# Hybrid trunk layer: which instructions behind the second hand-written order are tied to the order of the source

## The chip, the core and the metric

One core of one Trainium2 chip runs the kernel. Its engines work side by side, each in the order of its own instruction stream: TensorE (PE in the profile, its weight loads PEld) multiplies, VectorE (DVE), ScalarE (ACT) and GpSimd (POOL) do the elementwise work, and SyncE (SP) issues the DMA transfers. The metric is the device time of one execution in microseconds, the median over runs.

## The reference

One layer of a decoder trunk over 1024 tokens of width 1024, all in float32. The first half projects the normed input, runs stick-breaking attention (8 heads) beside a convolution module, and adds an output projection to x. The second half, in which the change lies, is a feed-forward network with a causal convolution of width 3 on its gate:

```python
h = rms_norm(x, norm2_g[layer])
gate, val = jnp.split(h @ w_up[layer], 2, axis=-1)
gate = jax.nn.silu(causal_depthwise_conv(gate, ffn_dw_w[layer], ffn_dw_b[layer]))
x = x + (gate * val) @ w_down[layer]
```

`w_up` is 1024 x 5632 and `w_down` 2816 x 1024.

## The kernel before

**Precision.** A float32 operand is split into a rounded high part (ScalarE, line 383: a cast) and the rest (VectorE or GpSimd, line 384: the operand minus its high part). A product of two operands is three matmuls (lines 387 to 389): high with high, high with low, low with high.

**The up-projection.** The 2816 gate columns and the 2816 value columns are worked in 22 blocks, f = 0 to 21. Block f takes 128 gate columns and 128 value columns, each 1024 long, that is a 2 x 2 arrangement: a11 and a12 are the two halves (512 rows each) of the gate columns, a21 and a22 those of the value columns. With the token side B cut in the same way, seven products take the place of eight. Besides a11, a12 and a22, four sums are operands; in `sums_up` they are made on GpSimd: S1 = a21 + a22 (line 1829), S3 = a11 - a21 (line 1830, written over a21), S2 = S1 - a11 (line 1831, over a11) and S4 = a12 - S2 (line 1835, over a12). Each is then split. In `up`, seven products of 12 matmuls each go to PSUM banks, and VectorE adds them into the gate g and the value v (lines 2000 to 2008; the first is copied by ScalarE, line 1999). Then come the gate's convolution (ScalarE at line 2009, two VectorE instructions at line 2011), Silu (ScalarE, line 2013), the product with the value (VectorE, line 2014), and a store to DRAM (line 2015). The profile calls the operands a11, a12, a22 `a` and the sums `aS`, the products `u` and `u_S`, the loaded weights `rawu`, S1 before its split `s`.

**Buffers.** Weights of even blocks are loaded to the two buffers raw0 and raw1, those of odd blocks to three buffers of the tag xt (line 1805). The gate half of block 1 is the exception: it lies in raw0. So the gate half of block 2 goes to raw0 when S4 of block 1 is split, and the value half of block 2 to raw1 when S4 of block 0 is split. Products use six PSUM banks of the tag z, those of a11 and a12 in the loop two of the tag bank.

**What sets the order.** The program is put in order when it is built, by a list scheduler with a timing estimate: an instruction that it holds ready may go ahead of one that stands earlier in the source. Two stretches are exempt: a `Plan` object emits its operations by a list of numbers (`ORDERS`), and `in_order` then ties each instruction of an engine to the one before it, which needs no semaphore but fixes the order of the stream. The second plan holds the output projection, the second norm, all seven products of block 0 with their additions (line 1928), and of block 1 the gate's load, the splits of a11 and a12 and their two products. It ends at line 1986. Behind it stands the loop over f:

```python
for f in range(NF):
    if f + 1 < NF:
        raw_next = load_up(f + 1)
    up(f, A)
    if f + 1 < NF:
        A = sums_up(f + 1, raw_next)
    if f == 0:
        in_order(start_at, last_planned, ORDERED[1:])
```

The call in its last line covers what the first turn emits: of `up(0)` only the convolution, Silu, product and store are left, and of `sums_up(1)` the four sums and the splits of S2, S1, S3, S4 and a22, in this order. On VectorE, ScalarE and GpSimd these are tied to each other in the order of the source and behind the last planned instruction of their engine. TensorE's and SyncE's streams are not tied there, nor is anything of block 2 and later, which the scheduler may put among or before them.

Of the kernel before, what the change touches and what calls it, by code (L numbers as in the profile page):

```python
# [40 lines left out]
ORDERED = (mybir.EngineType.PE, mybir.EngineType.DVE, mybir.EngineType.Activation, mybir.EngineType.Pool)  # L41
# [103 lines left out]
class Plan:  # L145
# [36 lines left out]
    def add(self, cost, *args):  # L182
        if not isinstance(cost, dict):
            cost, args = {cost: args[0]}, (lambda eng, f=args[1]: f(),) + args[2:]
        op = Plan.Op()
        op.shares = "DVE2" in cost
        op.cost, op.emit, op.key = {e.rstrip("2"): c for e, c in cost.items()}, args[0], args[1]
        op.after = list(args[2]) if len(args) > 2 else []
        op.takes = list(args[3]) if len(args) > 3 else []
        op.end, op.engine, op.n, op.moves = None, None, len(self.ops), [Plan.ROWS]  # L190
        self.ops.append(op)
        return op
# [77 lines left out]
def kernel(  # L270
# [21 lines left out]
    nc = tc.nc  # L292
# [169 lines left out]
    def part_of(big_tile, i, words):  # L462
        return big_tile[:, i * words:(i + 1) * words]

    def in_order(start_at, last=None, engines=ORDERED):
        last = {} if last is None else last
        for ins in nc.cur_bb.bb.instructions[start_at:]:
            if ins.engine in engines:
                if ins.engine in last:
                    tc.add_manual_dep(ins, last[ins.engine].name, mybir.DependencyInfo(  # L470
                        mybir.DependencyClass.NoSync, mybir.DependencyReason.DATA), reason="planned order")
                last[ins.engine] = ins
        return last

    start_at = len(nc.cur_bb.bb.instructions)
    g1 = []
# [796 lines left out]
    for h, half in [(h, half) for h in range(H) for half in range(2)]:  # L1273
# [38 lines left out]
        for g in (2 * half, 2 * half + 1):  # L1312
# [47 lines left out]
            last = None  # L1360
            if g % 2 == 0:
                po, pd = plan.token("o"), {}
            for sp in range(g + 1):
# [50 lines left out]
                last = add("PE", 480, products, k, [c] + v2 + ([last] if last else [prev_last] if g % 2 else []))  # L1414
# [203 lines left out]

    plan.run(ORDERS[0])
    in_order(start_at)  # L1620
    conv_ctx.close()
    ps_ctx.close()
# [18 lines left out]
    start_at = len(nc.cur_bb.bb.instructions)  # L1641
# [154 lines left out]
    def load_up(f):  # L1796

        both = []
        for b in (0, DFF):
            if f == 1 and b == 0:  # L1800
                both.append(next_raw[0])
                continue
            both.append(op.tile([P, ND, P], F32, tag="xt", name=f"rawu{f}_{b}", bufs=3) if f % 2 else
                        raw([P, ND, P], F32, f"rawu{f}_{b}"))
            nc.sync.dma_start(both[-1], w_up_k[:, :, b + f * P:b + (f + 1) * P])
        return both

    def sums_up(f, raws):

        A = {}  # L1810

        def both(name, src):
            if f == 1 and name in A_next:
                A[name] = A_next[name]
                return
            if name in ("11", "22"):
                tag, bufs = {"11": ("v", 2), "22": ("m", 1)}[name]
                t = op.tile([P, 2, 4, P], F32R, tag=tag, name=f"a{name}_{f}", bufs=bufs)
            else:
                t = whl([P, 2, 4, P], F32R, f"a{name}_{f}")  # L1820
            A[name] = (t[:, 0], t[:, 1])
            split(*A[name], src)

        (a11, a12), (a21, a22) = [(raw[:, :4, :], raw[:, 4:, :]) for raw in raws]
        s1 = op.tile([P, 4, P], F32, tag=f"t{f % 2 + 1}", name=f"s1_{f}")
        tt = nc.gpsimd.tensor_tensor
        both("11", a11)
        both("12", a12)
        tt(s1, a21, a22, op=ALU.add)  # L1829
        tt(a21, a11, a21, op=ALU.subtract)  # L1830
        tt(a11, s1, a11, op=ALU.subtract)
        both("S2", a11)
        both("S1", s1)
        both("S3", a21)
        nc.gpsimd.tensor_tensor(a12, a12, a11, op=ALU.subtract)  # L1835
        both("S4", a12)
        both("22", a22)
        return A
# [145 lines left out]
    gv, banks_of, A_next, next_raw = [], {}, {}, []  # L1984
    first_operands(FIRST)
    plan.run(ORDERS[1])
    last_planned = in_order(start_at)
    start_at = len(nc.cur_bb.bb.instructions)

    def up(f, A):  # L1990
        def product(a, b):
            return product_up(f, A, a, b)

        tt = nc.vector.tensor_tensor
        g, v = gv[f % 2], gv[2 + f % 2]
        y = op.tile([P, S], F32, tag="h2", name=f"y{f}", bufs=2)
        g0, g1, v0, v1 = g[:, :HS], g[:, HS:], v[:, :HS], v[:, HS:]
        if f > 1:
            nc.scalar.copy(v0, product("11", "11"))
            tt(g0, product("12", "21"), v0, op=ALU.add)  # L2000
        if f:
            tt(g1, product("S2", "T2"), v0, op=ALU.add)
            tt(v0, product("S3", "T3"), g1, op=ALU.add)
            p5 = product("S1", "T1")
            tt(g1, p5, g1, op=ALU.add)
            tt(v1, p5, v0, op=ALU.add)
            tt(g1, product("S4", "22"), g1, op=ALU.add)
            tt(v0, product("22", "T4"), v0, op=ALU.add)
        nc.scalar.activation(y, g, AF.Identity, scale=par("fw", (KF - 1) * NF + f), bias=par("fb", f))  # L2009
        for j in range(1, KF):  # L2010
            nc.vector.scalar_tensor_tensor(y[:, j:], g[:, :S - j], par("fw", (KF - 1 - j) * NF + f), y[:, j:],  # L2011
                                           op0=ALU.mult, op1=ALU.add)
        nc.scalar.activation(y, y, AF.Silu)
        tt(y, v, y, op=ALU.mult)
        nc.sync.dma_start(act_d[f], y)
# [4 lines that stand above are left out]
        up(f, A)  # L2020
        if f + 1 < NF:
            A = sums_up(f + 1, raw_next)
        if f == 0:
            in_order(start_at, last_planned, ORDERED[1:])

# [117 lines left out]
    for i in range(len(PAIRS)):  # L2145
        for n, name in enumerate(using if i else making):
# [7 lines left out]
            for s in range(4):  # L2154
# [4 lines left out]
                for j, ((ah, al), (bh, bl)) in enumerate(parts):  # L2159
                    first, last = begins and j == 0, j == len(parts) - 1  # L2160
# [42 lines left out]
```

## Time and profile before

| what | value |
| --- | --- |
| median of 3 runs | 1114.94 us (1114.22 to 1115.05) |
| the profiled execution's own time | 1115.21 us |
| its span, first to last instruction | 1112.9 us |
| busy: VectorE | 871.7 us (78%) |
| busy: ScalarE | 586.9 us (53%) |
| busy: GpSimd | 580.6 us (52%) |
| mean granted TensorE clock | 0.995 |
| DMA | 118.00 MB, mean 106 GB/s |

Times inside the kernel are counted from the span's start. The second plan ends, and the loop begins, at about 490 us; the loop's products run to about 900 us, and the down-projection fills the rest. TensorE's busy time and the chain of waits are shown where they are used. In a row of the timeline the first two numbers are start and duration; in square brackets stands how long the engine had been idle before it, and what ended that.

### The profile page before, as it was taken

What the parts mean: (1) busy time and instruction counts of PE and PEld (TensorE: products, weight loads), DVE (VectorE), ACT (ScalarE), POOL (GpSimd) and SP (SyncE); (2) the same over time, 40 slices, a digit from 0 to 9 for tenths busy, and PEclk for the clock granted to TensorE, in tenths of its full rate; (3) what the DMA queues carried; (4) which work ended last, traced back from release to release, by engine and by line L of the source; (5) the groups of instructions that cost most, each with busy time, mean ns of one, the idle gap of its engine ahead of it and who ended that gap; (6) DMA issues with size and microseconds to landing.
All of it is one profiled execution on the core that took longest, in us unless ns stands there. A gap on an engine that the chain in (4) does not pass through costs nothing.

```text
span 1112.9 us, 14818 instructions
## 1 busy us (share of the span) xinstructions
PE 1088.1 (98%) x5258; PEld 905.4 (81%) x5258; DVE 871.7 (78%) x1200; ACT 586.9 (53%) x1050; POOL 580.6 (52%) x496
## 2 busy tenths in 40 slices
PE   8999999999999999979999999999999999999998
PEld 5888878889898887857888888888888888888887
DVE  5488798789989886878876777677777678797785
ACT  6445466676766654734433434333333378676660
POOL 3177889874734324753433133223322189888770
PEclk9999999999999999998999999999999999999999
DMA  7121210343732434522322222213132482403404
GB/s 269 39 57 32 82 58 20 114 152 120 238 87 77 142 122 144 171 57 78 112 79 92 77 95 75 96 62 107 59 96 75 149 324 77 150 21 133 152 2 150
DMA packets 110504, 118.00 MB, mean 106 GB/s; under 512 B 21369, under 2 KB 90208, under 8 KB 110430
## 3 DMA queue, kind: packets, MB, share of 16 engines
q1 hardware_dynamic: 110414, 117.06, 32.0%
q8 instruction: 41, 0.67, 0.3%
q14 instruction: 33, 0.27, 0.1%
q10 hardware_dynamic: 16, 0.00, 0.0%
HBM read 82.43 MB, written 28.31 MB: 100 GB/s over the span
## 4 chain that ended last, share of the span: by engine, by line
PE 86%; POOL 4%; DVE 3%; DMA 3%; ACT 2%; issue 2%; SPq 0%; DVEq 0%; POOLq 0%; ACTq 0%
PE dn L2162 19%; PE u_S L387 7%; PE u_S L388 7%; PE u_S L389 7%; PE u L387 5%; PE u L389 5%; PE u L388 5%; PE po L1403 3%; PE wT L1375 3%; PE qk L387 3%; PE qk L389 3%; PE qk L388 3%; POOL attn L879 2%; PE z L1334 2%; PE z L1335 1%
## 5 line engine op out<-in xcount | busy, mean ns | idle before, releaser
L2162 PE MATMUL dn<-wd,wd 128*128 128x512 f32 x768 | 181.4, 389 | 0.0
L2162 PEld LDWEIGHTS dn<-wd,wd 128*128 128x128 f32 x768 | 144.2, 188 | 29.9
L387 PE MATMUL u_S<-bT,aS 128*128 128x512 f32 x264 | 103.9, 393 | 10.4 <-ACT aS L383 10.4
L388 PE MATMUL u_S<-bT,aS 128*128 128x512 f32 x264 | 103.4, 392 | 0.0
L389 PE MATMUL u_S<-bT,aS 128*128 128x512 f32 x264 | 102.8, 390 | 0.0
L2165 DVE TENSOR_TENSOR c<-dn,c 128x512 f32<-128x512 f32 x120 | 81.5, 686 | 26.7 <-PE dn L2162 26.1
L2067 ACT CAST wd<-rawd 128x512 fp32r<-128x512 f32 x128 | 72.5, 619 | 32.8 <-DMA rawd<-act_d 9.5
L383 ACT CAST aS<-rawu 128x512 fp32r<-128x512 f32 x63 | 38.8, 621 | 93.2 <-PE u_S L389 66.9
L1356 DVE TENSOR_TENSOR_SCAN nb<-nb,one 128x128 f32<-128x128 f32 (+7 forms) x64 | 84.6, 1340 | 0.6 <-ACT nb L1342 0.5
L1829 POOL TENSOR_TENSOR s<-rawu 128x512 f32<-128x512 f32 x21 | 28.8, 1370 | 107.6 <-DMA rawu<-in_w_up_dram 80.8
L2066 ACT COPY whole<-rawd 128x512 f32<-128x512 f32 x110 | 63.4, 586 | 24.2 <-DVE wd L2068 11.6
L1835 POOL TENSOR_TENSOR rawu<-rawu 128x512 f32<-128x512 f32 x21 | 28.9, 1374 | 80.6 <-DVE a L384 80.6
L2068 DVE TENSOR_TENSOR wd<-whole,wd 128x512 fp32r<-128x512 f32 x90 | 59.9, 684 | 13.5 <-ACT wd L2067 6.7
L387 PEld LDWEIGHTS u_S<-bT,aS 128*128 128x128 f32 x264 | 50.0, 190 | 21.7 <-ACT aS L383 11.4
L2011 DVE SCALAR_TENSOR_TENSOR y<-gv,cols_a,y 128x1023 f32<-128x1023 f32 (+1 forms) x44 | 58.3, 1326 | 10.5 <-ACT y L2009 10.4
L383 ACT CAST a<-rawu 128x512 fp32r<-128x512 f32 x61 | 37.7, 621 | 54.3 <-PE u_S L389 33.9
L389 PE MATMUL u<-b,a 128*128 128x512 f32 x168 | 65.5, 390 | 0.0
L387 PE MATMUL u<-b,a 128*128 128x512 f32 x168 | 65.4, 389 | 0.0
L388 PE MATMUL u<-b,a 128*128 128x512 f32 x168 | 65.4, 389 | 0.0
L388 PEld LDWEIGHTS u_S<-bT,aS 128*128 128x128 f32 x264 | 50.1, 190 | 10.3
L389 PEld LDWEIGHTS u_S<-bT,aS 128*128 128x128 f32 x264 | 49.7, 188 | 10.4
L384 DVE TENSOR_TENSOR a<-rawu,a 128x512 fp32r<-128x512 f32 x61 | 45.4, 746 | 16.0 <-ACT a L383 16.0
(382 smaller groups left out, 3204.9 us busy)
## 6 DMA issues: line engine op xcount, KB each, us to landing
rawu<-in_w_up_dram SPq DMA_DIRECT2D x44, 512.0 KB
act_d<-y SPq DMA_DIRECT2D x22, 512.0 KB
rawd<-act_d SPq DMA_DIRECT2D x22, 512.0 KB
rawd<-in_w_down_dram SPq DMA_DIRECT2D x22, 512.0 KB
raw_qk<-in_w_in_dram SPq DMA_DIRECT2D x16, 256.0 KB
rawo<-in_w_out_dram SPq DMA_DIRECT2D x8, 512.0 KB
m<-conv_d SPq DMA_DIRECT2D x16, 256.0 KB
xt<-in_x_dram SPq DMA_DIRECT2D x8, 512.0 KB
```

The costliest lines, as they stand in the source:

```text
L383: nc.scalar.copy(hi, src)
L384: lo_engine.tensor_tensor(lo, src, f32(hi), op=ALU.subtract)
L387: nc.tensor.matmul(ps, a_hi, b_hi, start=first, stop=False)
L388: nc.tensor.matmul(ps, a_hi, b_lo, start=False, stop=False)
L389: nc.tensor.matmul(ps, a_lo, b_hi, start=False, stop=last)
L1356: nc.vector.tensor_tensor_scan(rev, rev, ones_of[0][:, :w], 0.0, op0=ALU.mult, op1=ALU.max)
L2011: nc.vector.scalar_tensor_tensor(y[:, j:], g[:, :S - j], par("fw", (KF - 1 - j) * NF + f), y[:, j:], op0=ALU.mult, op1=ALU.add)
L2066: nc.scalar.copy(whole, src)
L2067: nc.scalar.copy(t[:, 0], src)
L2068: lo_engine.tensor_tensor(t[:, 1], whole, f32(t[:, 0]), op=ALU.subtract)
L2162: nc.tensor.matmul(ps, a[:, tok], b, start=first and m == 0, stop=last and m == 2, skip_group_check=True)
L2165: nc.vector.tensor_tensor(sums[c][s], ps, sums[c][s], op=ALU.add)
```

## The change

The second call of `in_order` is taken out, with the arguments that served it. The instructions of the two plans are tied as before, on all four engines. The first turn of the loop is no longer tied on VectorE, ScalarE and GpSimd: not among its own instructions, and not behind the planned ones. No instruction is added, taken away or altered.

```diff
-    def in_order(start_at, last=None, engines=ORDERED):
-        last = {} if last is None else last
+    def in_order(start_at):
+        last = {}
         for ins in nc.cur_bb.bb.instructions[start_at:]:
-            if ins.engine in engines:
+            if ins.engine in ORDERED:
                 if ins.engine in last:
                     tc.add_manual_dep(ins, last[ins.engine].name, mybir.DependencyInfo(
                         mybir.DependencyClass.NoSync, mybir.DependencyReason.DATA), reason="planned order")
                 last[ins.engine] = ins
-        return last
...
     plan.run(ORDERS[1])
-    last_planned = in_order(start_at)
-    start_at = len(nc.cur_bb.bb.instructions)
+    in_order(start_at)
...
         if f + 1 < NF:
             A = sums_up(f + 1, raw_next)
-        if f == 0:
-            in_order(start_at, last_planned, ORDERED[1:])
```

## The prediction, made before the result was known

> **What bounds the kernel now.** I read the page first, then the waits of TensorE, then a table by windows.
>
> ```profile
> PE 1088.1 (98%) x5258; PEld 905.4 (81%) x5258; DVE 871.7 (78%) x1200; ACT 586.9 (53%) x1050; POOL 580.6 (52%) x496
> ```
>
> TensorE is busy for 98% of the span, so time can only be won where it stands still or runs slowly. Its waits over the whole span (us in total, times, longest) say where:
>
> ```profile
> PE u_S L387 <- ACT aS L383: 10.4, 1, 10.4
> PE v L739 <- DVE lo_v L604: 1.9, 1, 1.9
> ```
>
> One wait is larger than all others, and it lies at the seam that the change touches. The windows (PE busy first, then its clock, DMA share and GB/s at the end):
>
> ```profile
> 492.74:503.33 10.59, 0.16 (x1) 0.00 (x0) 5.38 (x6) 4.75 (x6) 2.48 (x2) 0.69 0.00 0
> 503.33:508.86 5.53, 5.53 (x16) 4.13 (x17) 5.53 (x6) 2.04 (x4) 3.28 (x2) 0.68 0.28 104
> 508.86:899.80 390.94, 390.94 (x1726) 323.85 (x1725) 287.82 (x351) 149.25 (x216) 126.53 (x89) 1.00 0.30 98
> ```
>
> The reader is to see three things. From 492.74, when the next matmul was due, to 503.33 TensorE does nothing. For the next 5.53 us it is busy but slow. And then, over 391 us in which the scheduler alone set the order, it never pauses: 390.94 / 1726 = 0.2265 us a matmul. The chain that ended last shows what filled the hole:
>
> ```profile
> 487.53 5.15 DMA rawu<-in_w_up_dram
> 492.81 1.27 POOL s L1829
> 494.10 0.63 ACT aS L383
> 494.78 0.97 issue
> 495.76 0.69 DVE gv L1928
> 496.47 1.25 ACT y L2009
> 497.74 1.29 DVE y L2011
> 499.06 1.29 DVE y L2011
> 500.42 1.28 ACT L2013
> 501.72 1.06 ACT y L2013
> 502.77 0.52 ACT aS L383
> 503.33 0.79 PE u_S L387
> ```
>
> The last three lines are the point. The cast that TensorE waits for is block 1's first sum, and on ScalarE it stands behind block 0's Silu only because the source has it so; it needs nothing from the gate. The first lines show a second matter: the cast at 494.10 is of a sum S1, yet stands before line 2009. Block 1's casts are tied behind line 2009, so this one is block 2's, which the scheduler put ahead because its estimate held it ready. It waited for the load of 487.53.
>
> **The change part by part.** No instruction comes or goes; only the order is free. What goes is the tie of block 1's casts behind Silu. When could they have run?
>
> ```profile
> 487.46 1.30 POOL L1829 TENSOR_TENSOR s<-rawu 128x512 f32<-128x512 f32 x1
> 488.83 1.30 POOL L1830 TENSOR_TENSOR rawu<-rawu,rawu 128x512 f32<-128x512 f32 x1
> 490.21 1.29 POOL L1831 TENSOR_TENSOR rawu<-s,rawu 128x512 f32<-128x512 f32 x1
> 494.02 1.26 POOL L1835 TENSOR_TENSOR rawu<-rawu 128x512 f32<-128x512 f32 x1
> 494.10 0.62 ACT L383 CAST aS<-s 128x512 fp32r<-128x512 f32 x1 [9.96 <-POOL s L1829]
> 487.50 2.74 DVE L1928 TENSOR_TENSOR gv<-u_S,gv 128x512 f32<-128x512 f32 x4 [0.56 <-PE u_S L389]
> 494.75 1.08 DVE L384 TENSOR_TENSOR aS<-s,aS 128x512 fp32r<-128x512 f32 x1 [4.51 <-ACT aS L383]
> 503.95 0.68 DVE L384 TENSOR_TENSOR aS<-rawu,aS 128x512 fp32r<-128x512 f32 x1
> ```
>
> Block 1's S1, S3 and S2 are ready at 488.76, 490.13 and 491.50. ScalarE has been idle for 9.96 us at 494.10, so it is free from 484.14, and each cast takes 0.62: S1 488.8 to 489.4, S3 490.2 to 490.8, S2 491.5 to 492.15. All three high parts are there before 492.74. VectorE is free at 490.24 (487.50 + 2.74). Its three subtractions, one of 1.08 beside the last sum and two of 0.68, end by about 493.3 with the cast of S2 between, when the first low part is wanted at 492.74 + 2 x 0.2265 = 493.19 at the earliest. I count nothing for that 0.1.
>
> The terms are: the hole, 503.33 - 492.74 = 10.59; the slow matmuls, 5.53 us for 16 where 16 x 0.2265 = 3.62 would do, so 1.91. Sum 12.50, off the profiled execution's own 1115.21: **1102.71**. That execution is 0.27 above the median of the runs, so on their scale 1102.4.
>
> On the second term the Trainium skill, page "TensorE: Matmul & The Clock Gate", section "HAM oscillation", prices cold time at the throttled time times one minus the clock ratio. The 5.53 us at the row's mean clock of 0.68 would give 5.53 x 0.32 = 1.77 instead of 1.91, and 1102.6 on the runs' scale as an estimate by that page; I keep the row, which also holds the gaps between matmuls.
>
> What is late next, once the stall is gone? Block 1's five products then run from 492.74 to 492.74 + 60 x 0.2265 = 506.33, and the next operand is a11 of block 2. Its load needs raw0, so S4 of block 1 must be split first:
>
> ```profile
> 502.81 1.23 DVE L2014 TENSOR_TENSOR y<-gv,y 128x1024 f32<-128x1024 f32 x1 [2.46 <-ACT y L2013]
> 507.05 1.62 POOL L1830 TENSOR_TENSOR rawu<-rawu,rawu 128x512 f32<-128x512 f32 x1
> 507.44 1.77 DVE L384 TENSOR_TENSOR a<-rawu,a 128x512 fp32r<-128x512 f32 x1
> 507.55 0.37 SPq L1805 DMA_DIRECT2D rawu<-in_w_up_dram  x1
> 511.35 1.66 ACT L383 CAST a<-rawu 128x512 fp32r<-128x512 f32 x3 [5.99 <-DMA rawu<-in_w_up_dram]
> ```
>
> The load went out at 507.55 and its cast began at 511.35, 3.80 later. Even if block 2's S1 keeps its place before line 1835 on GpSimd, that line ends at 495.28, the cast at 495.9. VectorE is then in the two convolution steps (495.1 to 497.7, behind an addition at 493.9 and line 2009); with one more addition of 0.69 the subtraction is done by 499.2. Load 499.2, cast 503.0 to 503.6, first low part 504.3: 2 us before 506.33. It is the narrowest place, and goes into the range. The convolution and Silu of block 0 follow their last addition (about 494) in ScalarE's and VectorE's gaps, off the path: block 2 overwrites their buffers only after its first product, 506.33 + 2.72 = 509.05, and line 2009 to line 2014 take 1.25 + 2.58 + 1.28 + 1.06 + 1.23 = 7.4 us: 501.4 with nothing between, 507 with eight other VectorE operations of 0.69 between. Stores and loads on SyncE keep their data needs; a load queued behind that store is a rival below. Banks: after the four additions of 487.50 two of six z banks are occupied, so four products need no addition at all.
>
> The freedom also cuts the other way: block 1's sums may now go ahead of planned work.
>
> ```profile
> 482.26 1.78 DVE L1751 TENSOR_TENSOR bT<-t,bT 128x512 fp32r<-128x512 f32 x1
> 484.22 1.57 POOL L1751 TENSOR_TENSOR bT<-raws,bT 128x512 fp32r<-128x512 f32 x1 [0.73 <-ACT bT L1750]
> 485.76 1.74 POOL L1885 TENSOR_TENSOR aS<-rawu,aS 128x512 fp32r<-128x512 f32 x1
> 487.53 0.39 PE L388 MATMUL u<-bT,a 128*128 128x512 f32 x1
> ```
>
> S1 of block 1 uses the buffer of a token tile that VectorE reads until 484.04, so only these two GpSimd operations can be overtaken. Three sums of 1.30 before the first would end it at 484.04 + 3.90 + 1.57 = 489.5, where TensorE wants it at 487.53: at most 2.0 us lost, at least nothing. I take nothing, as the gap of 0.73 us before it is too short for one sum, and keep the 2.0 for the range.
>
> **The rivals.** *A sum holds the first low part.* Line 384 took 1.77 at 507.44, beside the GpSimd sum of 507.05, and 0.68 alone at 503.95. The change moves block 1's subtractions from a time when GpSimd was idle to beside its sums. If the one that TensorE wants first is held like this, it comes 1.77 - 0.68 = 1.1 us later: 1103.5. Against: GpSimd waited for a load from 491.5 to 492.8, just then, and TensorE can begin with whichever sum is complete. Chance 0.10. The Trainium skill, page "SBUF — State Buffer", section "SBUF: two separate sides", has the rule behind it: a VectorE operation with two SBUF inputs and a GpSimd operation that reads SBUF exclude each other for the whole instruction. By that rule the loss could be a whole sum, and the time 1103.7 as an estimate by the page; the 1.77 agrees with it.
>
> *A part of the hole stays, or moves to block 2.* The VectorE row at 494.75 shows the mechanism: block 2's subtraction, put early, held the queue for 4.51 us until its load had landed. If it stands ahead of block 1's subtractions, the first of these ends at 495.83 + 0.68 = 496.5, 3.3 us late, and the time is 1105.7. The clock need not fall in so short a hole: a mean of 0.69 over 10.59 us, if it went from full to half, means that it was full for the first 4.0 us. Or the load of block 2's gate stands behind block 0's store on SyncE: store by 504 to 506, cast at 508 to 510, a hole of 2 to 4 us, with the slow matmuls up to 6, so 1104.4 to 1108.4. For it: the estimate misjudged loads here. Against: 2 us of slack. Chance 0.20.
>
> *The order stays as it is*, because the scheduler also puts block 0's gate ahead of block 1's casts. Then nothing changes: 1114.9. Against it speaks that block 2's cast, later in the source, went ahead of that gate. Chance 0.05.
>
> *Slower: the loop runs short every turn.* The window 508.86 to 899.80 is full because the elementwise engines are ahead. A new order could put a wait into VectorE's queue in each of the 20 turns that follow.
>
> ```profile
> 543.00:562.00 19.00, 19.00 (x86) 15.73 (x85) 17.15 (x23) 7.90 (x11) 2.59 (x2) 1.00 0.35 109
> 581.00:600.00 19.00, 19.00 (x86) 15.73 (x85) 13.71 (x17) 7.05 (x10) 2.44 (x2) 1.00 0.26 83
> ```
>
> In the dense turn VectorE works 17.15 of 19.03 us (84 x 0.2265). A wait of 2.8 us there, shorter than the 4.51 at the seam, makes 19.95, 0.92 more than TensorE needs; 20 such turns cost 18.4, and the time is 1102.4 + 18.4 = 1120.8. It decides from 12.5 / 20 = 0.63 us a turn. Against it: the sparse turn needs 13.71, and during the hole the DMA share was 0.00, so the hole gave the loads no head start that would now be missing. Chance 0.12.
>
> **How the numbers follow.** Forecast (hole and slow matmuls gone, up to 2.0 us lost to overtaken work): 0.53, own range 1101.5 to 1104.4. A held subtraction 0.10, part stays 0.20, no change 0.05, slower 0.12. The range 1101 to 1110 takes in these three, with the 2.0 us of overtaken work and a stall with its slow clock, and leaves out 0.17 and a little of the tails. Faster by over 0.2% (about 2.2 us, what a measurement of this kernel can tell from no change) 0.83, within it 0.05, slower 0.12.
>
> **What would show it.** Right: TensorE's wait for the cast of line 383 is gone, its clock is 1.00 from 490 to 510, the casts of block 1's sums stand before line 2009 on ScalarE, and the loop's products, which ended at 899.8, end near 887. Wrong: a TensorE wait of 2 us or more between 484 and 512, above all before a11 of block 2; a wait at line 388 near 487 (overtaken planned work); or, if slower, idle TensorE in every turn behind 510.

## The result and the profile after

| | before | after |
| --- | --- | --- |
| median of 4 runs each | 1114.99 us (1114.22 to 1116.24) | 1102.62 us (1101.59 to 1105.56) |
| ratio | | 0.9892 [0.9871, 0.9914] |
| the profiled execution's own time | 1115.21 us | 1103.06 us |
| its span | 1112.9 us | 1101.3 us |
| mean granted TensorE clock | 0.995 | 0.998 |

The change makes the kernel faster by 1.1%. The diff takes out a few lines, so a line of the loop before is one or two lower after: 1829, 1831 and 1885 are now 1828, 1830 and 1884; 2009 and 2013 are 2007 and 2011. Busy times of the engines, from the page of after:

```profile
PE 1087.1 (99%) x5258; PEld 905.8 (82%) x5258; DVE 874.9 (79%) x1200; ACT 587.0 (53%) x1050; POOL 585.1 (53%) x496
```

The instructions are the same in number; only the span is 11.6 us shorter. TensorE's waits after (us in total, times, longest):

```profile
PE hT L555 <- DVE x_k L548: 3.3, 2, 2.7
...
PE u_S L389 <- DVE aS L1884: 0.6, 1, 0.6
```

The wait of 10.4 us for the cast of line 383 is gone, and the longest lies at the kernel's start. One wait is new at the seam: 0.6 us for a planned subtraction. The table by windows of after, the first two windows by the same clock times as the hole before (span, then PE, PEld, DVE, ACT, POOL busy, PE's clock, DMA share, GB/s):

```profile
484.00:492.74 8.74, 8.10 (x35) 6.04 (x34) 8.20 (x8) 1.86 (x3) 8.66 (x6) 1.00 0.38 111
492.74:503.33 10.59, 10.59 (x48) 8.79 (x47) 9.74 (x12) 5.09 (x8) 7.39 (x6) 1.00 0.37 108
508.86:887.30 378.44, 378.44 (x1671) 313.48 (x1670) 284.32 (x345) 144.48 (x210) 122.39 (x85) 1.00 0.30 98
```

Where TensorE stood for 10.59 us it now works throughout at full clock, and the loop behind it still never pauses: 378.44 / 1671 = 0.2265 us a matmul, as before. But in the first window it is busy 8.10 of 8.74 us, where in before it was busy for all of them: something is lost there that was not lost before. ScalarE's rows in after show the new order:

```profile
483.17 0.62 ACT L383 CAST aS<-s 128x512 fp32r<-128x512 f32 x1 [0.53 <-POOL s L1828]
486.55 0.62 ACT L383 CAST aS<-rawu 128x512 fp32r<-128x512 f32 x1 [1.07 <-POOL rawu L1829]
491.66 0.62 ACT L383 CAST aS<-rawu 128x512 fp32r<-128x512 f32 x1 [4.48 <-POOL rawu L1830]
...
499.37 1.25 ACT L2007 ACTIVATE y<-gv,cols_a 128x1024 f32<-128x1024 f32 x1 [2.22 <-DVE gv L1927]
```

Block 1's casts of S1, S3 and S2 run at 483.17, 486.55 and 491.66, and block 0's convolution (now line 2007) only at 499.37.

**A ledger by marks.** The time before block 0's first product, called the head here, varies from one execution to the next (464.5 to 466.4 over the ten profiles of this study), so the seam is measured between two marks of TensorE: block 0's first product, and the a11 product of block 2. First before, then after:

```profile
466.17 0.48 PE L387 MATMUL u<-b,a_first 128*128 128x512 f32 x1
...
518.83 0.39 PE L387 MATMUL u<-b,a 128*128 128x512 f32 x1
```

```profile
465.85 0.48 PE L387 MATMUL u<-b,a_first 128*128 128x512 f32 x1
...
507.21 0.39 PE L387 MATMUL u<-b,a 128*128 128x512 f32 x1
```

The seam takes 518.83 - 466.17 = 52.66 us before and 41.36 after: 11.30 less. The head gives 0.32, and the rest of the loop and the down-projection nothing: together 11.6, the difference of the spans. Around the span lie 2.31 us before and 1.76 after, so the two profiled executions differ by 12.15.

### The profile page after: what moved, and what is told of

The parts are those of the page before. It is cut to its first block, busy times and chain, and to the rows that moved or that the text cites. A ratio compares the mean times of both kernels' runs of the same rounds, so it can differ in the third digit from the quotient of the medians.

```text
span 1101.3 us, 14818 instructions
## 1 busy us (share of the span) xinstructions
PE 1087.1 (99%) x5258; PEld 905.8 (82%) x5258; DVE 874.9 (79%) x1200; ACT 587.0 (53%) x1050; POOL 585.1 (53%) x496
## 4 chain that ended last, share of the span: by engine, by line
PE 89%; POOL 3%; DVE 3%; DMA 2%; issue 2%; ACT 1%; SPq 0%; POOLq 0%; DVEq 0%; ACTq 0%
PE dn L2158 19%; PE u_S L389 7%; PE u_S L387 7%; PE u_S L388 7%; PE u L388 5%; PE u L389 5%; PE u L387 5%; PE po L1402 3%; PE wT L1374 3%; PE qk L387 3%; PE qk L389 3%; PE qk L388 3%; POOL attn L878 2%; PE z L1333 2%; PE z L1334 1%
## 5 line engine op out<-in xcount | busy, mean ns | idle before, releaser
L389 PEld LDWEIGHTS u_S<-bT,aS 128*128 128x128 f32 x264 | 49.6, 188 | 11.3 <-DVE aS L1884 1.1
L1830 POOL TENSOR_TENSOR rawu<-s,rawu 128x512 f32<-128x512 f32 x21 | 31.4, 1494 | 47.9 <-DVE a L384 47.2
```

Of the source, the lines that this page charges most:

```text
L389: nc.tensor.matmul(ps, a_lo, b_hi, start=False, stop=last)
```

## The experiments

The open questions were these. Is the hole ScalarE's tie alone, as the chain of waits shows it (theory A), or VectorE's as well (theory B)? Is the slow stretch behind the hole the clock's or something else's? What does block 2's early S1 cost? And what did the free order give away? Each kernel is the one before with the edit shown, and each time stands beside runs of before on the same chip.

**Only ScalarE free.**

```diff
-            in_order(start_at, last_planned, ORDERED[1:])
+            in_order(start_at, last_planned, (ORDERED[1], ORDERED[3]))
```

> Only ScalarE is freed in the first turn; VectorE and GpSimd stay tied in the order of the source. If the tie on ScalarE alone made the hole (theory A), the casts of block 1 run at 489 to 492 and most of the 12.5 us goes: about 1103. If both ties did (theory B), block 1's subtractions still stand behind block 0's product of line 2014 on VectorE, which ended at 504.0: TensorE can only do the high parts early (10 matmuls of 0.2265 us for five products, two each), then waits until about 504.6 and is slow again. It then gains some 1 to 2 us: 1113 to 1114.

Measured: 1114.21 us, ratio 0.9993 [0.9984, 1.0002]; the seam 51.76, 0.90 less than before, with the time just outside theory B's 1113 to 1114. The timelines of ScalarE, VectorE and TensorE in this kernel, the row of each that matters:

```profile
490.58 0.62 ACT L383 CAST aS<-rawu 128x512 fp32r<-128x512 f32 x1 [0.75 <-POOL rawu L1831]
...
501.53 1.22 DVE L2014 TENSOR_TENSOR y<-gv,y 128x1024 f32<-128x1024 f32 x1 [2.46 <-ACT y L2013]
502.68 0.68 DVE L384 TENSOR_TENSOR aS<-rawu,aS 128x512 fp32r<-128x512 f32 x1
...
503.42 0.80 PE L389 MATMUL u_S<-bT,aS 128*128 128x512 f32 x1 [7.47 <-DVE aS L384]
```

The casts of the three sums are done by 491.2, where TensorE waited for one at 502.77 before, and nearly nothing is won: block 1's subtractions stand behind line 2014 on VectorE, and TensorE waits for them in place of the cast. Theory A falls. The chain of waits had named the wait that ended last, and a second one, on VectorE, ended only a little earlier.

**ScalarE and VectorE free, GpSimd tied.**

```diff
-            in_order(start_at, last_planned, ORDERED[1:])
+            in_order(start_at, last_planned, (ORDERED[3],))
```

> ScalarE and VectorE are freed, GpSimd stays tied behind the planned operations. In the changed kernel two sums of block 1 went ahead of planned GpSimd work, and block 1's first matmul began at 493.61, in a run that was 0.38 us ahead at 459, where the kernel before had ended its planned matmuls for 492.74. If that overtaking costs 1.25 us (theory), block 1 begins at about 492.7 here and the time is about 1101.4 on the scale of the changed kernel's 1102.6. If GpSimd's freedom is what brings the sums in time (rival), a wait of a few us comes back before block 1 and the time is 1104 to 1107.

Measured: 1104.81 us, 0.9905 [0.9886, 0.9924]. The hole before block 1 is gone, so the two ties together made it. The seam takes 40.24 us, 1.12 less than after, as the theory expected, but block 2 loses more than that. So the time falls into the rival's range, though the rival's wait before block 1 is not there. TensorE, VectorE, SyncE's queue, GpSimd and ScalarE in this kernel:

```profile
492.09 0.40 PE L387 MATMUL u_S<-bT,aS 128*128 128x512 f32 x1
...
495.32 1.77 DVE L384 TENSOR_TENSOR aS<-s,aS 128x512 fp32r<-128x512 f32 x1
497.02 1.78 DVE L384 TENSOR_TENSOR aS<-rawu,aS 128x512 fp32r<-128x512 f32 x1
...
498.83 0.37 SPq L1805 DMA_DIRECT2D rawu<-in_w_up_dram  x1
...
505.64 1.61 POOL L1831 TENSOR_TENSOR rawu<-s,rawu 128x512 f32<-128x512 f32 x1 [0.70 <-DVE a L384]
...
508.38 0.62 ACT L383 CAST aS<-rawu 128x512 fp32r<-128x512 f32 x1
...
509.43 2.32 DVE L2014 TENSOR_TENSOR y<-gv,y 128x1024 f32<-128x1024 f32 x1
...
513.47 0.68 DVE L384 TENSOR_TENSOR aS<-rawu,aS 128x512 fp32r<-128x512 f32 x1
...
514.20 0.50 PE L389 MATMUL u_S<-bT,aS 128*128 128x512 f32 x1 [2.40 <-DVE aS L384]
```

Block 2's S1 (the row with `s`, 495.32) is split ahead of block 1's S4 (497.02). The load of block 2's gate needs that split and goes out at 498.83. S2 of block 2, made from it, follows late: GpSimd sums it at 505.64, ScalarE casts it at 508.38, and its subtraction comes behind line 2014 and two additions, at 513.47. TensorE waits 2.40 us for it. In after S4 of block 1 is split first, and the same load is out earlier:

```profile
495.37 0.37 SPq L1804 DMA_DIRECT2D rawu<-in_w_up_dram  x1
```

So a free GpSimd costs 1.1 us ahead of block 1, and here its tie costs 2.4 at block 2.

**Each instruction of the first turn only behind the plan.** They are free among themselves, but may not overtake planned work.

```diff
-            in_order(start_at, last_planned, ORDERED[1:])
+            for ins in nc.cur_bb.bb.instructions[start_at:]:
+                if ins.engine in ORDERED[1:]:
+                    tc.add_manual_dep(ins, last_planned[ins.engine].name, mybir.DependencyInfo(
+                        mybir.DependencyClass.NoSync, mybir.DependencyReason.DATA), reason="planned order")
```

> The first turn's instructions are free among themselves, but all stand behind the last planned instruction of their engine. On VectorE the last planned additions stood behind block 2's early subtraction, which waited for its load until 494.75; block 1's subtractions then come after 496.4 plus 0.6. If that early subtraction is harmful by itself (theory), TensorE does 10 high-part matmuls to about 495.0 and waits about 2 to 2.5 us for the first low part at 497.1 to 497.6: 1104.5 to 1105.5. If only the order of gate and casts mattered (rival), the time is that of the changed kernel, 1102.6, or up to 1.2 less.

Measured: 1106.31 us, 0.9922 [0.9907, 0.9937]; the seam 44.74. The expectation (up to 1105.5) is missed by 0.8 us, by a term that it did not hold, the clock. VectorE and TensorE in this kernel:

```profile
494.40 1.09 DVE L384 TENSOR_TENSOR aS<-s,aS 128x512 fp32r<-128x512 f32 x1 [4.59 <-ACT aS L383]
...
495.64 0.50 PE L387 MATMUL u_S<-b,aS 128*128 128x512 f32 x1 [1.80 <-ACT aS L383]
...
497.34 0.50 PE L389 MATMUL u_S<-bT,aS 128*128 128x512 f32 x1 [0.46 <-DVE aS L384]
```

The mechanism is the one that the prediction named as a rival: block 2's subtraction, put early, holds VectorE until its load has landed (4.59 us), and what TensorE needs stands behind it. The two waits are 2.26 us together. Then the clock falls to half for 3.41 us; its windows stand in the last section.

**TensorE kept busy in the hole.** 36 matmuls whose product nobody reads are added to fill it, and everything else is tied in the order of the source, TensorE's stream as well.

```diff
+        if f == 0:
+            idle = psz.tile([P, 512], F32, tag="z", name="idle_up")
+            for _ in range(36):
+                nc.tensor.matmul(idle, ident_r, B["22"][0][:, 0, :], start=True, stop=True)
         up(f, A)
...
-            in_order(start_at, last_planned, ORDERED[1:])
+            in_order(start_at, last_planned)
```

> The kernel before with 36 additional matmuls, whose product nobody reads, put behind the planned ones on TensorE: 36 x 0.2265 = 8.2 us of the 10.6 us hole are filled, and block 1's operands come as late as before. If the slow 5.53 us after the hole come from the clock that fell during it (theory), the clock stays 1.00 and the 16 matmuls take 3.6 us: about 1.9 us less than before, 1113.1. If they were slow because low parts came late (rival), the 5.53 us stay and the time is 1115.0. If the filling matmuls hold up block 1 (they should end near 501.0, before 503.3), it is more.

Measured: 1114.43 us, 0.9994 [0.9985, 1.0004]; the time alone tells nothing. The trace does. Windows over the filled hole and over the 16 matmuls that were slow before:

```profile
492.50:503.00 10.50, 8.72 (x38) 6.69 (x36) 5.37 (x6) 4.73 (x6) 2.48 (x2) 1.00 0.00 0
503.04:507.50 4.46, 4.15 (x17) 3.14 (x18) 4.46 (x6) 2.03 (x4) 2.41 (x2) 1.00 0.29 118
```

The clock stays at 1.00, and the first 16 matmuls take 4.34 us (503.04 to 507.38) where they took 5.53. So of the slow term of 1.91 us, 1.19 is the clock's. The remaining 0.72 is there at full clock as well: block 1's operands come one by one at this place, and at 504.08 TensorE stops again, for the next cast. The seam is 51.32, 1.34 less than before; besides those 1.19 the hole is 0.22 shorter (492.67 to 503.04); what made it so is not shown.

**Only block 2 held back.** The tie of before stays, and block 2's splits and sums must stand behind the last instruction of the first turn on their engine.

```diff
+            start_at_2 = len(nc.cur_bb.bb.instructions)
             A = sums_up(f + 1, raw_next)
         if f == 0:
-            in_order(start_at, last_planned, ORDERED[1:])
+            last_of = in_order(start_at, last_planned, ORDERED[1:])
+        if f == 1:
+            for ins in nc.cur_bb.bb.instructions[start_at_2:]:
+                for to in {e: [last_of[e]] for e in ORDERED[1:]}.get(ins.engine, ()):
+                    tc.add_manual_dep(ins, to.name, mybir.DependencyInfo(
+                        mybir.DependencyClass.NoSync, mybir.DependencyReason.DATA), reason="planned order")
```

> The kernel before with its tie kept; block 2's sums, casts and subtractions are put behind the first turn on the three engines, so that its early S1 no longer stands before block 0's last additions and line 2009. Theory: those additions come at 493.1 instead of 495.76, line 2009, Silu and block 1's casts come 2.6 us earlier, and the 10.6 us hole shrinks to 8: from the first product of block 0 to block 2's a11 it takes 52.66 - 2.6 = 50.0 us, and the time is 1112.3. Rival: block 2's early sum cost nothing by itself, since the additions had to wait for something else: 1115.0.

Measured: 1111.56 us, 0.9973 [0.9963, 0.9984]; the seam 49.94. VectorE and TensorE:

```profile
491.89 0.69 DVE L1928 TENSOR_TENSOR gv<-u_S,gv 128x512 f32<-128x512 f32 x1 [2.70 <-PE u_S L389]
...
499.48 0.80 PE L387 MATMUL u_S<-bT,aS 128*128 128x512 f32 x1 [7.63 <-ACT aS L383]
```

Block 0's last two additions, which began at 495.76 before, behind block 2's subtraction, begin here at 491.89, as soon as the product is done, and 2.72 us of the seam go, close to the expected 2.6. The hole had two causes in a row: block 2's early S1, worth 2.7 us, which delayed the gate; and the order of the source, which put block 1 behind the gate.

**Both improvements together.** If overtaken planned work and block 2's early S1 are what is left, then a version without either should show neither wait. The first kernel ties GpSimd only (as in the second experiment), the second everything behind the plan (as in the third). In both, block 2's GpSimd work stands behind S4 of block 1 (line 1835) and block 2's VectorE work behind the last planned addition and block 1's last two subtractions; the diff is the first kernel's.

```diff
+            start_at_2 = len(nc.cur_bb.bb.instructions)
             A = sums_up(f + 1, raw_next)
         if f == 0:
-            in_order(start_at, last_planned, ORDERED[1:])
+            turn = {e: [i for i in nc.cur_bb.bb.instructions[start_at:] if i.engine == e] for e in ORDERED[1:]}
+            plan_end = dict(last_planned)
+            in_order(start_at, last_planned, (ORDERED[3],))
+        if f == 1:
+            for ins in nc.cur_bb.bb.instructions[start_at_2:]:
+                for to in {ORDERED[1]: [plan_end[ORDERED[1]]] + turn[ORDERED[1]][-2:], ORDERED[3]: turn[ORDERED[3]][-1:]}.get(ins.engine, ()):
+                    tc.add_manual_dep(ins, to.name, mybir.DependencyInfo(
+                        mybir.DependencyClass.NoSync, mybir.DependencyReason.DATA), reason="planned order")
```

> As the run with ScalarE and VectorE free and GpSimd tied, but block 2's S1 stands behind line 1835 of block 1 on GpSimd, and on VectorE behind block 0's last additions and block 1's subtractions. Theory: that run lost 2.4 us before a low part of block 2 because block 2's S1 held up S4 of block 1 and so the load of block 2's gate, which went out at 498.83 against 495.37 in the changed kernel. Here the load goes out at about 495, no wait is left, and it is 40.2 us from block 0's first product to block 2's a11 (41.36 in the changed kernel, 52.66 before): 1101.5. Rival: VectorE has too much to do at that place whatever the order of block 2's S1, and a wait of 2 to 3 us before block 2's low parts stays: 1104 to 1105.

> As the run with the first turn free but behind the planned instructions, with block 2's S1 held back as in the run beside this. Theory: the 4.5 us that that run stood above its neighbours (44.74 us from block 0's first product to block 2's a11, against 40.24) came from block 2's subtraction standing before the last planned additions. Without it block 1's first low part is ready at 493.8 + 0.6 = 494.4 to 495, and TensorE has high parts for 10 matmuls, to 495.0: 40.2 to 40.8 us, 1101.5 to 1102.1. Rival: the additions themselves hold the subtractions up, and 2 us or more stay: 1104 and more.

Measured: 1102.60 us, 0.9892 [0.9875, 0.9908], and 1102.58 us, 0.9894 [0.9879, 0.9909]. What is left of TensorE's wait in block 2, in the first kernel and in the second:

```profile
512.66 0.50 PE L389 MATMUL u_S<-bT,aS 128*128 128x512 f32 x1 [0.19 <-DVE aS L384]
```

```profile
512.59 0.50 PE L389 MATMUL u_S<-bT,aS 128*128 128x512 f32 x1 [0.71 <-DVE aS L384]
```

The waits do most of what was expected of them: 2.40 becomes 0.19 with GpSimd tied, and behind the plan nothing is left ahead of block 1, but a wait of 0.71 is left in block 2. The times do not: 1101.5, and 1101.5 to 1102.1, were expected, and neither time can be told from the changed kernel's. By the marks they are 0.81 and 0.24 us shorter than after up to block 3, less than the head's scatter of 1.8.

**The changed kernel once more,** on the chip of the last three.

> The changed kernel again, beside the others on one chip: 1102.6, and 41.4 us from block 0's first product to block 2's a11.

Measured: 1102.58 us, 0.9893 [0.9878, 0.9908]. Its seam is 41.37 where the first profile had 41.36, and the wait for line 1884 is there again (0.7 us where it was 0.6). So between these two executions, a single pair, the seam repeats to a hundredth, and what varies is the head. All kernels by the marks:

| kernel | first product | to block 2's a11 | to block 3's a11 | median, us |
| --- | --- | --- | --- | --- |
| before | 466.17 | 52.66 | 71.70 | 1114.99 |
| after | 465.85 | 41.36 | 60.40 | 1102.62 |
| after, once more | 464.52 | 41.37 | 60.41 | 1102.58 |
| only ScalarE free | 465.07 | 51.76 | 70.80 | 1114.21 |
| ScalarE and VectorE free | 465.50 | 40.24 | 61.98 | 1104.81 |
| behind the plan | 465.69 | 44.74 | 63.78 | 1106.31 |
| hole filled | 466.04 | 51.32 | 70.36 | 1114.43 |
| block 2 held | 465.39 | 49.94 | 68.98 | 1111.56 |
| ScalarE, VectorE free, block 2 held | 466.35 | 40.06 | 59.59 | 1102.60 |
| behind the plan, block 2 held | 465.71 | 40.12 | 60.16 | 1102.58 |

An undisturbed turn takes 19.04 us, the difference of the two columns where block 2 loses nothing.

## Why the prediction was right

The forecast was 1102.4 us, and the runs gave 1102.62. The mechanism held; one term was mis-sized, and others that have nothing to do with the change made up for most of it.

**What bounds the kernel: right.** The hole at the seam was the largest thing to be had, and it went whole, in the one stage and nowhere else: the loop's rate is the same to the fourth digit. But the chain of waits named one cause where there were two. The prediction counted VectorE free at 490.24 without saying that this, too, hung on the tie being off. It was off in this change, so the number is right; with ScalarE alone freed, 0.9 us of the seam went. And 2.7 us of the hole hung on block 2's early S1, which the free order takes off the path as well.

**The sum of 12.50: right as what the seam can give.** Taken off 52.66 it leaves 40.16. The two kernels that neither overtake planned work nor let block 2 go early have 40.06 and 40.12. The slow term, 1.91, is real as a sum. The text put it down to slow matmuls; by the kernel with the hole filled, 1.19 of it was the clock and 0.72 operands that came one by one, and in the free order both go. The rule for cold time of the Trainium skill (page "TensorE: Matmul & The Clock Gate", section "HAM oscillation") gave an estimate of 1.77 for it, which is nearer to the whole than to the clock's own share of 1.19; the row was the better choice for the sum.

**Nothing for overtaken work: wrong, by 1.2 us.** This is the step that failed: "S1 of block 1 uses the buffer of a token tile that VectorE reads until 484.04, so only these two GpSimd operations can be overtaken", and of the 0 to 2.0 us it took nothing. GpSimd in after:

```profile
481.31 1.83 POOL L1828 TENSOR_TENSOR s<-rawu 128x512 f32<-128x512 f32 x1
483.10 1.73 POOL L1787 TENSOR_TENSOR raws<-raws,t 128x512 f32<-128x512 f32 x1
484.79 1.73 POOL L1829 TENSOR_TENSOR rawu<-rawu,rawu 128x512 f32<-128x512 f32 x1
486.49 1.74 POOL L1750 TENSOR_TENSOR bT<-raws,bT 128x512 fp32r<-128x512 f32 x1
488.18 1.74 POOL L1884 TENSOR_TENSOR aS<-rawu,aS 128x512 fp32r<-128x512 f32 x1
```

S1 of block 1 (line 1828) runs at 481.31, before VectorE reads the token tile that was named (481.90 to 483.68 in after). The premise had the wrong tile: by the source S1 of block 1 lies in a buffer of the tag t2, which the token tile of line 1785 (of before) uses, and VectorE was done with that one at 478.83 in before; the tile read until 484.04 has the tag t1. So S1 goes ahead of the planned line 1787, and S3 (line 1829) ahead of lines 1750 and 1884. Three operations are overtaken, not two. Most of the price was paid on VectorE, not on GpSimd where the prediction looked for it:

```profile
483.61 1.77 DVE L1884 TENSOR_TENSOR aS<-rawu,aS 128x512 fp32r<-128x512 f32 x1
485.30 1.77 DVE L1884 TENSOR_TENSOR a<-rawu,a 128x512 fp32r<-128x512 f32 x1
```

In before the first of these ran at 483.96 and took 0.68, with GpSimd idle when it began (from 483.49 to 484.22):

```profile
483.96 0.68 DVE L1885 TENSOR_TENSOR aS<-rawu,aS 128x512 fp32r<-128x512 f32 x1
```

Now it begins while GpSimd is at line 1787 (1788 in before), which S1 has pushed back from 481.66 to 483.10. It takes 1.77, and TensorE waits for it:

```profile
485.43 0.50 PE L389 MATMUL u_S<-bT,aS 128*128 128x512 f32 x1 [0.63 <-DVE aS L1884]
...
488.28 0.50 PE L388 MATMUL u<-bT,a 128*128 128x512 f32 x1
...
493.61 0.39 PE L387 MATMUL u_S<-bT,aS 128*128 128x512 f32 x1
```

Block 1 begins at 493.61, where 492.74 less the head's 0.32 would be 492.42: 1.19 us are lost. The stop at 485.43 is 0.78 of them (1.01 from the matmul before, where 0.2265 is the rate), a smaller one at 488.28 is 0.18, where line 388 begins just as GpSimd ends the overtaken line 1750 at 488.23, and the rest lies in single matmuls that follow at slightly more than the rate. That overtaking is the cause is shown by the kernels in which GpSimd's planned work cannot be overtaken: three of them have no such loss, with seams of 40.24, 40.06 and 40.12.

**Why the total fits nevertheless.** 12.50 was forecast for the profiled execution; the seam gave 12.50 - 1.2 = 11.3. The head gave 0.32 and the time around the span 0.55, both by chance of these two executions, so 12.15. The medians differ by 12.37. A part of the agreement is luck, of the size of the head's scatter.

**The narrowest place: a11 right, and one step too short.** The load of block 2's gate was put at 499.2 with 2 us to spare. In after it is out at 495.37, and block 2 loses nothing. With GpSimd tied it goes out at 498.83, close to the forecast, and a11 itself is in time, as forecast: its product follows block 1's last without a gap. But the prediction stopped there. S2, which is made from a11, comes later still, and its low part is where TensorE waits 2.40. The change was spared that because the scheduler happened to split S4 of block 1 first, an order better than the one assumed.

**The rivals.** The held subtraction was right as a mechanism (0.68 to 1.77) but struck a planned subtraction at 483.61, not block 1's first low part. "A part of the hole stays, or moves to block 2" did not happen in the change, but the third experiment is it (block 2's subtraction held VectorE for 4.59 us), and the second is its form within block 2. Its remark that the clock need not fall in a hole of 3.3 us does not hold for every hole: in the third experiment it fell with waits of 1.80 and 0.46. No turn of the loop ran short, so the slower rival is out: the window from 508.86 shows it. The order did not stay as it was.

**The signs.** The wait is gone, the clock is 1.00 from 484, the casts of block 1 stand before the convolution, and the loop's products end at about 888. The sign for overtaken work was to be a wait at line 388 near 487. It came there at 488.28, but with 0.18 only; the larger stop is at line 389, at 485.43.

## What to carry to other kernels

The chain of waits names the tie that ended last; before you price its removal, see what else the waiting engine needs and whether that is queued behind the same thing, since freeing ScalarE alone was worth 0.9 us of 11.3. When an order written by hand is loosened, look at both sides: what may now come earlier, and which planned work it can overtake or slow down by running beside it. To price a change at one seam, measure between two marks of the bounding engine: in the one kernel profiled twice the seam repeated to a hundredth of a microsecond, while the times of its runs lie up to four apart (1101.59 to 1105.56).

## What the hardware showed unexpectedly

**The clock changes on a fixed grid, and waits shorter than one step of it can be enough to drop it.** In the trace's record of the granted clock, the stretches that do not run past the end of a kernel are multiples of 3.413 us (10.24 of half clock at the hole before, 6.83 with block 2 held, 3.41 behind the plan). One such step is called a cell here. The windows below are cut at that grid; the counts in brackets take in a matmul that began before the window and reaches into it. Behind the plan:

```profile
494.49:497.90 3.41, 1.80 (x6) 1.08 (x7) 3.41 (x6) 1.86 (x2) 0.45 (x1) 1.00 0.00 0
497.90:501.32 3.42, 3.42 (x10) 2.64 (x9) 3.42 (x3) 0.00 (x0) 3.21 (x2) 0.50 0.01 2
```

With the hole filled:

```profile
499.57:502.98 3.41, 1.66 (x8) 1.00 (x6) 0.95 (x2) 2.85 (x4) 0.00 (x0) 1.00 0.00 0
502.98:506.40 3.42, 3.05 (x12) 2.24 (x13) 3.42 (x5) 2.09 (x5) 1.39 (x1) 1.00 0.38 153
```

ScalarE and VectorE free, at the wait in block 2:

```profile
509.10:512.52 3.42, 2.69 (x12) 1.88 (x11) 3.42 (x4) 2.17 (x4) 1.56 (x1) 1.00 0.01 2
512.52:515.93 3.41, 1.73 (x8) 1.43 (x9) 3.41 (x5) 0.00 (x0) 1.60 (x1) 1.00 0.38 154
```

Behind the plan TensorE begins six matmuls in the first cell, where 15 fit at full rate, and the next cell runs at half clock. With the hole filled, and at the wait in block 2, the clock stays at 1.00. The longest single wait does not decide: 1.80 us dropped the clock, while 1.81 with the hole filled and 2.40 in block 2 did not (all three lay across two cells). PE's busy time in these rows, 1.80 against 1.66 and 1.73, does not order them either. Nor does the number of matmuls: the row with the hole filled counts eight, but two of them had begun before the cell, so that six began in it as well. What within a cell decides stays open. The Trainium skill, page "TensorE: Matmul & The Clock Gate", Part 1, gives a free-running window of 3413 ns, with which the record agrees. Its section "HAM oscillation" gives "no PE-idle gaps >~3.4µs" as the rule; here the clock fell with no idle gap above 1.80 us, so that keeping every gap below the page's figure is no safety.

**A subtraction on VectorE can more than double beside work on GpSimd.** The same instruction took 0.68 us when GpSimd was idle as it began, and 1.77 when it began within GpSimd's line 1787. GpSimd's sums S1 and S3 take 1.83 and 1.73 there, where they took 1.30 each in before. Both engines pay, and in after VectorE's busy time over the span is 3.2 us higher, GpSimd's 4.5 us, with the same instructions.
